# A hybrid state-space and attention layer on one core: spread row splits, moved sums, other queues for stores, a third weight set, two more dummy products

## The chip, the core and the metric

The kernel runs on one core of a Trainium2 chip. Five engines work side by side, each through its own instructions in order: TensorE (PE in the profile), VectorE (DVE), ScalarE (ACT), GpSimd (POOL) and SyncE (SP), which here only issues transfers between the chip's memory (DRAM) and on-chip memory. Engines and transfers wait for each other by semaphores. The metric is the device time of one execution in microseconds (us); lower is better.

## The reference

One step of a one-layer streaming encoder for 1024 prompt rows and 64 sample rows (T = 1088 columns in the kernel, which holds everything transposed), in float32. Cut to what matters:

```python
xn = rmsnorm(x, norm_mix_w)
z, xbc, dt, q, k, v, gate_ssm, gate_att = split(xn @ w_in)
xs, B, C = split(silu(causal_conv(xbc)))          # width 4
y = rmsnorm_groups((ssd_scan(xs, dt, B, C) + d * xs) * silu(z))
o = rmsnorm_heads(softmax(q1 k1) v - lam * softmax(q2 k2) v)   # 8 heads, rope on q and k
x = x + (sigmoid(gate_ssm) * (y @ w_ssm) + sigmoid(gate_att) * (o @ w_att)) @ w_out
ha, hb = split(rmsnorm(x) @ w_up)                  # 2 x 2816
x = x + (silu(causal_conv(ha)) * hb) @ w_down      # width 3
```

The caches of the sample stream enter attention, scan and convolutions; keys, values, states and convolution rows are outputs too.

## The kernel before, in words

*Products.* Each float32 operand is split into a rounded high part and the low rest, by a cast on ScalarE (`w_hi`, `hi`) and a subtraction on DVE (`w_lo`, `lo`). A product of two matrices is three passes: high by high, high by low, low by high (L159 to L161). The 1088 columns are cut into 384, 384 and 320 (`WIDE`). A product of 8 blocks of 128 and one such piece is 24 passes into one PSUM bank; an evacuation on ScalarE or DVE then frees the bank. Weights come as `w_f` by a load of 512 KB (L144), into pools with two sets; `extra`, where there is one, gives a third set, used in every third turn.

*Start.* The mean square of the input's rows is made on TensorE with a matrix of ones. Ahead of its products, products of ones by ones, whose result nothing reads, are put in by the table `IDLE`: nine ahead of the first mean square and eight behind it.

*Attention (some 350 to 1090 us).* Eight heads run over nine blocks of query rows. For each head SyncE loads `q_t`, the high and low keys `kh_t` and `kl_t` (three slots each), the caches `ch_t`, `cl_t`, `cv_t`, and the values `v_t`. Between the steps of attention a *filler* runs: the input projection's products for the gates (`gate_tiles`), for z (`z_tiles`) and for the convolution (`conv_tiles`), in the order of `ORDER`, at 1.9 pieces per step (`ATT_STEPS`). Their results go to DRAM as `g_sc`, `z_sc` and `x_sc`. The tiles `gt` and `zr` share three slots (`staged`). These stores are issued by SyncE in the same queue as the loads; only those of the first two entries of `ORDER` by GpSimd (`early`).

*Scan (some 1090 to 1350 us).* The state-space scan works over groups and chunks: loads of `in`, `zin` and, per chunk, a broadcast `bc` of 512 KB; exponentials on ScalarE, products on TensorE. The filler goes on between its steps, first the last z and gate tiles, then the two products that follow attention and the first ssm product. The second ssm product (`branch(stage, side, y_sc[D:], wbs[1], ...)`) comes behind the scan.

*FFN (some 1720 us to the end).* Up and down projections are made by a scheme with 7 products of blocks rather than 8. 22 *units* of the up projection (number i = 0 to 21 in the list `work`) each make one tile of `ha` and `hb`; 12 units of the down projection follow, in three groups of four (i = 22 to 25, 26 to 29, 30 to 33) over 8, 8 and 6 blocks of the 22. A unit has seven parts in the order b11, t2, b21, t3, t1, t4, b22, each for two halves s: 14 *piles* of products. A pile of the first two groups has 12 passes, of the last 9. The weights of the next unit are combined on GpSimd (`left_parts`, L1180 to L1193, tiles `ws`) and split. The hidden rows come back from DRAM (`q_sc`): *hidden sums* (`hidden_sums`, L1248 to L1251, tiles `gb`, `ge`) make the four t parts out of the four b parts, for one pair of tiles at a time, on GpSimd, with four loads and four stores; *hidden parts* (`hidden_part`, L1262 to L1264) load each part for a group (`hr`) and split it by a cast and a subtraction for each load. When the last unit of a group runs, the 14 parts of the next group are queued in `to_come` as the tiles that they go into become free, two after every second pile; `hidden_next` takes one from the queue after each pile and pins its instructions behind the last evacuations of PSUM (`emptied`).

*What sets the order.* A scheduler places the instructions of each engine by priorities and its own estimate of times; `tc.issue_after(x)` holds what is written under it behind x. A transfer from SyncE or ScalarE takes one of eight completion semaphores in turn and waits until the transfer before it on that semaphore has landed; the two engines share the eight. GpSimd's transfers have eight others.

Of the kernel before, what the change touches and what calls it, by code (L numbers as in the profile page):

```python
# [46 lines left out]
QR = 10  # L47
QSQ = 1
QUICK = 400
IDLE = (9, 8)  # L50
AT = 4
AHEAD_IN = 100
AHEAD = 100
# [23 lines left out]
def hybrid_layer(ctx: ExitStack, tc: tile.TileContext, xT, xN, prm, cst, rope, wvd, win, wbs, wba, wout, wup, wdn,  # L77
# [51 lines left out]

    xn = rows_by_part("xn")  # L130
    extra, turn, ahead, quick, asked, decayed, lowered = None, 0, AHEAD_IN, QUICK, None, None, None
    emptied, produced, early, early_w = (None, None), None, False, 0

    def raw_weights(block, k, m, pool=None):
        nonlocal turn, early_w
# [103 lines left out]
    def run(gen):  # L239
        for _ in gen:  # L240
            pass
# [349 lines left out]
    def gate_tiles(tiles):  # L591
        for j in tiles:
            def evac(ps, c, w):
                nonlocal last_gate
                gt = staged("gt")[:, :w]
                last_gate = act(gt, ps, AF.Tanh, scale=0.5)
                (G.dma_start if early else load)(out=g_sc[P * j : P * (j + 1), c : c + w], in_=gt)

            yield from project(win[B_G + j], evac)

    def z_tiles(tiles):
        for j in tiles:
            def evac(ps, c, w):
                zr = staged("zr")[:, :w]
                act(zr, ps, AF.Tanh, scale=0.5)
                V.scalar_tensor_tensor(zr, zr, 1.0, ps, ALU.add, ALU.mult)  # L606
                (G.dma_start if early else load)(out=z_sc[P * j : P * (j + 1), c : c + w], in_=zr)

            yield from project(win[B_Z + j], evac)

    def conv_tiles(tiles):
        for f in tiles:
            tail = None

            def evac(ps, c, w):
                nonlocal tail
                n = min(w, TP - c)
                pre = cv_pool.tile([P, 387], F32, name="pre", tag="pre", bufs=2)
                cc = cv_pool.tile([P, 384], F32, name="cc", tag="cc", bufs=3)
# [12 lines left out]
                cw = lambda i: col(O_CW + 4 * f + i)  # L632
                act(cc[:, :m], pre[:, :m], AF.Identity, bias=col(O_CB + f), scale=cw(0))  # L633
                for i in range(1, 4):
                    V.scalar_tensor_tensor(cc[:, :m], pre[:, i : i + m], cw(i), cc[:, :m], ALU.mult, ALU.add)  # L635
                act(pre[:, :m], cc[:, :m], AF.Tanh)
                V.scalar_tensor_tensor(cc[:, :m], pre[:, :m], 1.0, cc[:, :m], ALU.add, ALU.mult)
                load(out=x_sc[P * f : P * (f + 1), c : c + n], in_=cc[:, :n])
                if n < w:
                    load(out=x_sc[P * f : P * (f + 1), c + n : c + w], in_=cc[:, n + 3 : m])  # L640

            yield from project(win[B_X + f], evac)

    def stream():
        nonlocal early, early_w
        early_w = 10
        for n, (kind, which) in enumerate(ORDER):
            early = n < 2
# [16 lines left out]
    with (tc.tile_pool(name="ak", bufs=1) as ak, tc.tile_pool(name="at", bufs=1) as at,  # L665
# [159 lines left out]
        for h in range(8):  # L825
# [22 lines left out]
            run(last)  # L848
            late = [lambda h=h, o=o_t, q=ssq, s=s0: head_out(h, o, q, s)]
        late[0]()  # L850


    with (tc.tile_pool(name="sin", bufs=1) as sin, tc.tile_pool(name="sp", bufs=1) as sp,
# [183 lines left out]
    def mixed(m, c, t):  # L1037
        w = t.shape[1]
        for q in range(c // QW, -(-(c + w) // QW)):
# [2 lines left out]
            S.copy(hi, t[:, a - c : b - c])  # L1042
            V.tensor_tensor(out=lo, in0=t[:, a - c : b - c], in1=hi, op=ALU.subtract)

    run(branch(stage, side, y_sc[D:], wbs[1], 0, (n_sc, m_sc), mixed, parts, loaded))
    bs.release()
    xn_pool.release()

# [110 lines left out]
    def left_halves(blocks):  # L1159
# [6 lines left out]
        for h in range(2):  # L1166
            for r in range(2):
                yield own(halves[r][h])

    def left_parts(blocks, tag="fs"):  # L1170

        n = blocks[0].shape[1] // 2
        a = []
        for block in blocks:
# [14 lines left out]
        for i, src in enumerate((s1, q22)):  # L1189
            hi, lo = (x[:, 512 * i : 512 * i + n] for x in t)  # L1190
            split(hi, lo, src)
            yield hi, lo
        G.tensor_tensor(out=s2, in0=q12, in1=s2, op=ALU.subtract)  # L1193
        hi, lo = (wp.tile([P, WMAX], R32, name=name, tag=name, bufs=2)[:, :n] for name in ("w_hi", "w_lo"))
        split(hi, lo, s2)
        yield hi, lo
# [66 lines left out]
            S.copy(hi[:, j : j + n], t)  # L1263
            V.tensor_tensor(out=lo[:, j : j + n], in0=t, in1=hi[:, j : j + n], op=ALU.subtract)  # L1264

    to_come = []

    def hidden_next():
        if to_come:
            with tc.issue_after(emptied[0].ins), tc.issue_after(emptied[1].ins):  # L1270
                hidden_part(*to_come.pop(0))

    def piles(i, nk):
        banks = {}
# [208 lines left out]
    for i, (g, f) in enumerate(work[2:], 2):  # L1483
# [20 lines left out]
        for p, s in [(p, s) for p in ((0, 2, 1, 3, 4, 5, 6) if i == 2 else range(7)) for s in range(2)]:  # L1504
            u.send((p, s))
            hidden_next()
            if s == 1:
                more_left(i + 1)
                if last or i == FT - 2 and PARTS[p] in ("t2", "t3", "t4"):
                    to_come.extend((0 if i == FT - 2 else work[i + 1][0], PARTS[p], u) for u in range(2))  # L1510
                if p == 3 and i < FT + 2 and i % 2 == 0:
                    hidden_sums(i // 2 - 1)
        if i + 1 < len(work):
            left.setdefault(i + 1, []).extend(coming)
        del left[i]
# [108 lines left out]
```

## Time and profile before

| what | us |
|---|---|
| median of three runs | 2449.74 |
| lowest and highest of them | 2444.35, 2454.61 |
| the profiled execution | 2450.37 |
| its span | 2448.6 |
| TensorE busy in it | 2424.2 |
| DVE, ScalarE, GpSimd busy | 1603.0, 1141.4, 678.4 |

The profiled execution's own time is 1.8 us longer than its span, which runs from the first to the last recorded instruction. In the rows of a profile, L1283 is line 1283 of the kernel; `out<-in` names the tiles; PE is TensorE, SPq the queue of SyncE. "Idle before, releaser" is how long the engine did nothing ahead of the row and what ended that.

### The profile page before, as it was taken

How to read it: one execution, taken by the hardware profiler on the slowest of the kernel's cores; microseconds unless marked ns; L12 is line 12 of the kernel's file. 1: busy time of each engine (PE TensorE's matmuls, PEld its weight loads, DVE VectorE, ACT ScalarE, POOL GpSimd, SP SyncE). 2: the span in 40 equal slices, each digit the busy share in tenths (PEclk: the TensorE clock that was granted, in tenths of full speed). 3: DMA queues.
4: the chain of work that ended last, by engine and by line, in shares of the span. 5: the costliest groups of instructions: out<-in, count | busy, mean ns of one | idle time of the engine just before them, and what ended most of it. 6: DMA issues, size and time to landing. Idle time of an engine off the chain costs nothing.

```text
span 2448.6 us, 44619 instructions
## 1 busy us (share of the span) xinstructions
PE 2424.2 (99%) x16956; PEld 2351.5 (96%) x16956; DVE 1603.0 (65%) x2755; ACT 1141.4 (47%) x2497; POOL 678.4 (28%) x723
## 2 busy tenths in 40 slices
PE   9999999999999999999999999999999999999998
PEld 8999999999999999998889999999999999999998
DVE  7426255855787667546757784756877777786766
ACT  6334344644665555437664553224544433353542
POOL 0000011100100101004433334003366676655434
PEclk9999999999999999999999999999999999999999
DMA  4218158554444354255789765655143343467774
GB/s 173 82 57 290 61 208 270 148 154 142 126 149 131 116 158 121 91 170 173 218 261 318 226 193 186 196 182 181 54 143 126 121 139 116 153 206 202 212 185 155
DMA packets 267783, 403.55 MB, mean 165 GB/s; under 512 B 33296, under 2 KB 199696, under 8 KB 267440
## 3 DMA queue, kind: packets, MB, share of 16 engines
q1 hardware_dynamic: 254544, 376.99, 48.6%
q0 software_dynamic: 6960, 16.98, 3.4%
q10 hardware_dynamic: 6064, 6.72, 0.8%
q8 instruction: 133, 2.18, 0.4%
q14 instruction: 82, 0.67, 0.1%
HBM read 267.04 MB, written 133.56 MB: 164 GB/s over the span
## 4 chain that ended last, share of the span: by engine, by line
PE 90%; DVE 3%; DMA 3%; ACT 2%; issue 1%; POOL 0%; SPq 0%; ACTq 0%; DVEq 0%; POOLq 0%
PE mx L1283 17%; PE mm L159 13%; PE mm L161 13%; PE mm L160 12%; PE mm L1283 7%; PE mx L159 5%; PE mx L161 5%; PE mx L160 5%; PE po L776 3%; PE sc L729 2%; DMA hr<-q_sc 2%; PE sc L728 2%; PE pt L757 1%; PE mx L1343 1%; PE yi L902 1%
## 5 line engine op out<-in xcount | busy, mean ns | idle before, releaser
L159 PE MATMUL mm<-xn_hi,w_hi 128*128 128x384 f32 (+1 forms) x1416 | 471.0, 333 | 0.0
L161 PE MATMUL mm<-xn_hi,w_lo 128*128 128x384 f32 (+1 forms) x1416 | 468.3, 331 | 0.4 <-DVE w_lo L152 0.4
L160 PE MATMUL mm<-xn_lo,w_hi 128*128 128x384 f32 (+1 forms) x1416 | 467.7, 330 | 0.0
L159 PEld LDWEIGHTS mm<-xn_hi,w_hi 128*128 128x128 f32 x1416 | 266.7, 188 | 4.0 <-issue 1.6
L161 PEld LDWEIGHTS mm<-xn_hi,w_lo 128*128 128x128 f32 x1416 | 266.5, 188 | 3.7 <-issue 1.5
L160 PEld LDWEIGHTS mm<-xn_lo,w_hi 128*128 128x128 f32 x1416 | 266.7, 188 | 2.5 <-issue 1.1
L152 DVE TENSOR_TENSOR w_lo<-w_f,w_hi 128x1024 fp32r<-128x1024 f32 x116 | 147.0, 1269 | 110.0 <-ACT w_hi L151 109.4
L1283 PE MATMUL mx<-n,wh 128*128 128x272 f32 x1076 | 207.5, 290 | 0.7 <-ACT u L1427 0.5
L1283 PE MATMUL mx<-m,w_hi 128*128 128x272 f32 x1010 | 193.0, 289 | 4.6 <-DVE down L1441 4.6
L151 ACT CAST w_hi<-w_f 128x1024 fp32r<-128x1024 f32 x116 | 121.4, 1048 | 147.8 <-PE mm L160 89.8
L1283 PEld LDWEIGHTS mx<-n,wh 128*128 128x128 f32 x1076 | 170.5, 190 | 1.4 <-ACT u L1427 1.1
L1283 PEld LDWEIGHTS mx<-m,w_hi 128*128 128x128 f32 x1010 | 159.3, 189 | 5.3 <-issue 2.8
L1283 PE MATMUL mx<-n,wl 128*128 128x272 f32 x538 | 156.2, 290 | 0.0
L159 PE MATMUL mm<-b_hi,w_hi 128*128 128x384 f32 (+1 forms) x448 | 145.9, 327 | 0.6 <-DVE b_g L227 0.6
L1283 PE MATMUL mx<-m,w_lo 128*128 128x272 f32 x505 | 146.1, 289 | 0.0
L161 PE MATMUL mm<-b_hi,w_lo 128*128 128x384 f32 (+1 forms) x448 | 144.8, 324 | 0.6 <-DVE w_lo L152 0.6
L160 PE MATMUL mm<-b_lo,w_hi 128*128 128x384 f32 (+1 forms) x448 | 145.0, 324 | 0.0
L742 ACT ACTIVATE p_t<-sc,mx 128x1024 f32<-128x1024 f32 (+5 forms) x144 | 106.3, 739 | 75.9 <-DVE mx L733 34.1
L635 DVE SCALAR_TENSOR_TENSOR cc<-pre,par,cc 128x384 f32<-128x384 f32 (+1 forms) x216 | 126.4, 586 | 15.6 <-ACT cc L633 13.3
L623 POOL COPY pre<-pre 128x3 f32<-128x3 f32 x48 | 14.6, 304 | 353.5 <-DVE sm L745 121.7
L1068 ACT CAST w_hi<-ws 128x512 fp32r<-128x512 f32 (+1 forms) x62 | 37.6, 606 | 149.3 <-PE mx L1283 96.8
L159 PE MATMUL mx<-xn_hi,w_hi 128*128 128x384 f32 (+1 forms) x312 | 104.8, 336 | 2.2 <-DVE zr L606 2.2
(420 smaller groups left out, 6649.3 us busy)
## 6 DMA issues: line engine op xcount, KB each, us to landing
w_f<-in_win_dram SPq DMA_DIRECT2D x67, 512.0 KB, 4.0
w_f<-in_wup_dram SPq DMA_DIRECT2D x44, 512.0 KB, 3.8
hr<-q_sc SPq DMA_DIRECT2D x70, 272.0 KB, 5.0
bc<-a_sc SPq DMA_DIRECT2D x32, 512.0 KB, 5.9
q_sc<-hb SPq DMA_DIRECT2D x44, 272.0 KB, 2.3
gb<-q_sc SPq DMA_DIRECT2D x44, 272.0 KB, 3.7
x_sc<-cc SPq DMA_DIRECT2D x48, 192.0 KB, 1.9
q_sc<-gb SPq DMA_DIRECT2D x33, 272.0 KB, 2.4
```

The source lines that it names most:

```text
L151: S.copy(hi, w)
L152: lowered = V.tensor_tensor(out=lo, in0=w, in1=hi, op=ALU.subtract)
L159: PE.matmul(ps, a_hi, b_hi, start=i == 0, stop=False)
L160: PE.matmul(ps, a_hi, b_lo, start=False, stop=False)
L161: produced = PE.matmul(ps, a_lo, b_hi, start=False, stop=i == n - 1)
L635: V.scalar_tensor_tensor(cc[:, :m], pre[:, i : i + m], cw(i), cc[:, :m], ALU.mult, ALU.add)
L728: PE.matmul(ps[:n, a : a + b], lhs, r_hi, start=True, stop=False)
L729: PE.matmul(ps[:n, a : a + b], lhs, r_lo, start=False, stop=True)
L742: act(p_t[:n, :nk], sc[c][:n, :nk], AF.Exp, bias=mx[:n, c : c + 1], accum_out=dst)
L776: PE.matmul(po[:n, :P], a_t[b // 4][:kw, b % 4 * P : b % 4 * P + n], rhs, start=b == 0, stop=b == nb - 1)
L1068: S.copy(hi, src)
L1283: PE.matmul(ps, w[x][:, c], b[y][:, k], start=start and k == t == 0, stop=k == nk - 1 and t == 2, skip_group_check=not start)
```

## The change: what it does

Five edits. `IDLE` becomes (11, 8). The stores of the filler's tiles go through `send`: GpSimd until the end of attention, ScalarE after it. A pool `wx2` gives a third weight set during the second ssm product. The last hidden sums (the eleventh pair of tiles) leave the first unit of the down projection, behind its fourth part, for the third unit (i = 24), behind its sixth part, pinned behind the subtraction on GpSimd that ends that unit's weight sums. `hidden_next` lets two parts go for every three piles.

```diff
-IDLE = (9, 8)
+IDLE = (11, 8)
...
-    emptied, produced, early, early_w = (None, None), None, False, 0
+    emptied, produced, send, early_w = (None, None), None, G.dma_start, 0
...
-                (G.dma_start if early else load)(out=g_sc[P * j : P * (j + 1), c : c + w], in_=gt)
+                send(out=g_sc[P * j : P * (j + 1), c : c + w], in_=gt)
...
-                (G.dma_start if early else load)(out=z_sc[P * j : P * (j + 1), c : c + w], in_=zr)
+                send(out=z_sc[P * j : P * (j + 1), c : c + w], in_=zr)
...
-                load(out=x_sc[P * f : P * (f + 1), c : c + n], in_=cc[:, :n])
+                send(out=x_sc[P * f : P * (f + 1), c : c + n], in_=cc[:, :n])
                 if n < w:
-                    load(out=x_sc[P * f : P * (f + 1), c + n : c + w], in_=cc[:, n + 3 : m])
+                    send(out=x_sc[P * f : P * (f + 1), c + n : c + w], in_=cc[:, n + 3 : m])
...
         late[0]()
+        send = S.dma_start
...
+    extra = tc.alloc_tile_pool(name="wx2", bufs=1, side="right")
     run(branch(stage, side, y_sc[D:], wbs[1], 0, (n_sc, m_sc), mixed, parts, loaded))
+    extra.release()
+    extra = None
...
-        G.tensor_tensor(out=s2, in0=q12, in1=s2, op=ALU.subtract)
+        summed = G.tensor_tensor(out=s2, in0=q12, in1=s2, op=ALU.subtract)
...
+    to_come, owed = [], 0
...
     def hidden_next():
+        nonlocal owed
         if to_come:
-            with tc.issue_after(emptied[0].ins), tc.issue_after(emptied[1].ins):
-                hidden_part(*to_come.pop(0))
+            owed += 2
+            if owed >= 3:
+                owed -= 3
+                with tc.issue_after(emptied[0].ins), tc.issue_after(emptied[1].ins):
+                    hidden_part(*to_come.pop(0))
...
-                if p == 3 and i < FT + 2 and i % 2 == 0:
+                if p == 3 and i < FT and i % 2 == 0:
                     hidden_sums(i // 2 - 1)
+                elif (i, p) == (FT + 2, 5):
+                    with tc.issue_after(summed.ins):
+                        hidden_sums(FT // 2 - 1)
```

Over the whole program SyncE has 902 rows for 1079, GpSimd 784 for 647 and ScalarE 2006 for 1972. Lines behind the edits move by up to 13 (L1264 becomes L1270, L1441 becomes L1451).

The queue of SyncE in attention, where the loads of a head's queries and keys are issued. Before:

```order
L597 DMA g_sc<-gt 128x320
L144 DMA w_f<-in_win_dram 128x1024
L672 DMA kh_t<-k_st 64x1088
L672 DMA q_t<-q_st 64x1088 x2
L672 DMA kh_t<-k_st 64x1088
L672 DMA kl_t<-k_st 64x1088 x2
L672 DMA q_t<-q_st 128x1088
L672 DMA kh_t<-k_st 64x1088 x2
L597 DMA g_sc<-gt 128x384
L672 DMA kl_t<-k_st 64x1088 x2
L597 DMA g_sc<-gt 128x384
L692 DMA cv_t<-in_cv_dram 128x4x128
```

The same place in the queue of SyncE now:

```order
L144 DMA w_f<-in_win_dram 128x1024
L671 DMA kh_t<-k_st 64x1088
L671 DMA q_t<-q_st 64x1088 x2
L671 DMA kh_t<-k_st 64x1088
L671 DMA kl_t<-k_st 64x1088 x2
L671 DMA q_t<-q_st 128x1088
L671 DMA kh_t<-k_st 64x1088 x2
L671 DMA kl_t<-k_st 64x1088 x2
L691 DMA cv_t<-in_cv_dram 128x4x128
```

The three stores of `g_sc` have left it; the loads keep their order among themselves.

The queue of GpSimd in the first units of the down projection, where the weight sums (`ws`, `w_f`), the hidden sums (`ge`, `gb`) and the adding stores of the results (`down`) stand. Before:

```order
L1180 TENSOR_TENSOR ws_24596<-w_f 128x512
L1448 DMA out_dram<-down 128x544
L1181 TENSOR_TENSOR ws_24597<-ws_24596,w_f 128x512
L1186 TENSOR_TENSOR w_f<-w_f 128x512
L1248 TENSOR_TENSOR ge<-gb_24720,gb_24719 128x544
L1193 TENSOR_TENSOR ws_24597<-w_f,ws_24597 128x512
L1249 TENSOR_TENSOR gb_24720<-gb_24722,gb_24720 128x544
L1250 TENSOR_TENSOR gb_24719<-gb_24722,ge 128x544
L1448 DMA out_dram<-down 128x544 x2
L1251 TENSOR_TENSOR gb_24721<-gb_24721,gb_24719 128x544
L1448 DMA out_dram<-down 128x544
```

The same place now, up to the hidden sums two units later:

```order
L1187 TENSOR_TENSOR ws_24593<-ws_24592,w_f 128x512
L1192 TENSOR_TENSOR w_f<-w_f 128x512
L1199 TENSOR_TENSOR ws_24593<-w_f,ws_24593 128x512
L1458 DMA out_dram<-down 128x544 x3
L1186 TENSOR_TENSOR ws_24858<-w_f 128x512
L1187 TENSOR_TENSOR ws_24859<-ws_24858,w_f 128x512
L1192 TENSOR_TENSOR w_f<-w_f 128x512
L1199 TENSOR_TENSOR ws_24859<-w_f,ws_24859 128x512
L1254 TENSOR_TENSOR ge<-gb_25264,gb_25263 128x544
L1458 DMA out_dram<-down 128x544
L1255 TENSOR_TENSOR gb_25264<-gb_25266,gb_25264 128x544
```

The hidden sums no longer stand between the first down unit's weight sums, but behind those of the third.

The queue of SyncE at the start of the last group of the down projection, with loads of the hidden parts (`hr`), of earlier results (`xr`) and of weights (`w_f`). Before:

```order
L1262 DMA hr<-q_sc 128x544
L1262 DMA hr<-q_sc 128x272
L1417 DMA xr<-out_dram 128x544 x4
L1176 DMA w_f<-in_wdn_dram 128x768
L1262 DMA hr<-q_sc 128x544
L1262 DMA hr<-q_sc 128x272
L1262 DMA hr<-q_sc 128x544
L1262 DMA hr<-q_sc 128x272
L1417 DMA xr<-out_dram 128x544
```

The same place now:

```order
L1268 DMA hr<-q_sc 128x544
L1268 DMA hr<-q_sc 128x272
L1427 DMA xr<-out_dram 128x544 x4
L1268 DMA hr<-q_sc 128x544
L1268 DMA hr<-q_sc 128x272
L1182 DMA w_f<-in_wdn_dram 128x768
L1268 DMA hr<-q_sc 128x544
L1268 DMA hr<-q_sc 128x272
L1268 DMA hr<-q_sc 128x544
L1268 DMA hr<-q_sc 128x272
L1268 DMA hr<-q_sc 128x544
L1268 DMA hr<-q_sc 128x272
```

Behind the four loads of `xr` there stood the loads of two hidden parts; now six follow, the last two (rows behind those shown) around a store of `down`.

More of the change, by code (lines that the diff above doesn't have):

```diff
@@ L637, in evac @@
                 V.scalar_tensor_tensor(cc[:, :m], pre[:, :m], 1.0, cc[:, :m], ALU.add, ALU.mult)
-                load(out=x_sc[P * f : P * (f + 1), c : c + n], in_=cc[:, :n])
+                send(out=x_sc[P * f : P * (f + 1), c : c + n], in_=cc[:, :n])
                 if n < w:
-                    load(out=x_sc[P * f : P * (f + 1), c + n : c + w], in_=cc[:, n + 3 : m])
+                    send(out=x_sc[P * f : P * (f + 1), c + n : c + w], in_=cc[:, n + 3 : m])
             yield from project(win[B_X + f], evac)
     def stream():
-        nonlocal early, early_w
+        nonlocal early_w
         early_w = 10
-        for n, (kind, which) in enumerate(ORDER):
-            early = n < 2
+        for kind, which in ORDER:
             yield from {"c": conv_tiles, "z": z_tiles, "g": gate_tiles}[kind](which)
@@ L1168, in left_halves @@
                 yield own(halves[r][h])
+    summed = None
     def left_parts(blocks, tag="fs"):
+        nonlocal summed
         n = blocks[0].shape[1] // 2
@@ L1264, in hidden_part @@
             V.tensor_tensor(out=lo[:, j : j + n], in0=t, in1=hi[:, j : j + n], op=ALU.subtract)
-    to_come = []
+    to_come, owed = [], 0
     def hidden_next():
+        nonlocal owed
         if to_come:
-            with tc.issue_after(emptied[0].ins), tc.issue_after(emptied[1].ins):
-                hidden_part(*to_come.pop(0))
+            owed += 2
[3 more added lines that the diff above has]
+                    hidden_part(*to_come.pop(0))
     def piles(i, nk):
```

## Prediction

> **What bounds the kernel now.** I read the page first (busy shares and the chain of work that ended last), then the waits of TensorE, then the granted clock in stretches of 50 us, then the rows around each wait.
>
> ```profile
> span 2448.6 us, 44619 instructions
> ...
> PE 2424.2 (99%) x16956; PEld 2351.5 (96%) x16956; DVE 1603.0 (65%) x2755; ACT 1141.4 (47%) x2497; POOL 678.4 (28%) x723
> ...
> POOL 0000011100100101004433334003366676655434
> ...
> PE 90%; DVE 3%; DMA 3%; ACT 2%; issue 1%; POOL 0%; SPq 0%; ACTq 0%; DVEq 0%; POOLq 0%
> ```
>
> TensorE is busy for 2424.2 of 2448.6 us and is 90% of the chain. The work is a list of products that the change leaves as it is, so an edit can win only what TensorE loses between them: 24.4 us of idle time, and what a lower clock adds to the busy time. The profiled execution took 2450.4 us, span 2448.6; it lies 0.7 us above the median of the three runs, 2449.7. The runs spread from 2444.4 to 2454.6, so I call 0.5%, 12.2 us, the limit of what can be told from no change: faster means under 2437.5, slower over 2462.0.
>
> The waits of TensorE (total, times, longest, in us) that the change can reach:
>
> ```profile
> PE mx L1283 <- DVE down L1441: 4.6, 2, 2.6
> ...
> PE mx L159 <- DVE zr L606: 2.2, 1, 2.2
> ...
> PE st L315 <- DVE ns L315: 1.1, 1, 1.1
> ...
> PE mm L161 <- DVE w_lo L152: 1.0, 2, 0.6
> ```
>
> Two waits of the down projection, 2.6 and 2.0 us, are the largest. Some waits cost twice. Stretches of 50 us (the first number behind the five busy times is the granted clock):
>
> ```profile
> 500.00:550.00 50.00, 47.59 (x299) 44.85 (x298) 27.28 (x58) 22.81 (x66) 1.10 (x2) 0.97 0.57 154
> ...
> 1100.00:1150.00 50.00, 47.76 (x343) 42.10 (x343) 33.34 (x38) 35.18 (x90) 23.58 (x16) 1.00 0.54 168
> ...
> 2200.00:2250.00 50.00, 48.00 (x368) 47.57 (x368) 36.56 (x48) 18.44 (x36) 27.70 (x24) 0.97 0.87 236
> ...
> 2350.00:2400.00 50.00, 47.26 (x365) 46.84 (x364) 38.72 (x73) 23.93 (x54) 19.20 (x18) 0.97 0.85 234
> ```
>
> TensorE in attention (start, length, in brackets the idle time before and its releaser):
>
> ```profile
> 532.22 0.47 PE L728 MATMUL sc<-kh_t,q_t 128*128 128x512 f32 x1 [1.08 <-DMA kh_t<-k_st]
> ...
> 532.87 0.34 PE L159 MATMUL mm<-xn_hi,w_hi 128*128 128x384 f32 x1
> ...
> 533.04 0.34 PE L160 MATMUL mm<-xn_lo,w_hi 128*128 128x384 f32 x1
> ...
> 534.88 0.60 PE L729 MATMUL sc<-kl_t,q_t 128*128 128x512 f32 x1 [1.33 <-DMA kl_t<-k_st]
> ...
> 536.13 0.52 PE L159 MATMUL mm<-xn_hi,w_hi 128*128 128x384 f32 x1
> ...
> 536.45 0.52 PE L160 MATMUL mm<-xn_lo,w_hi 128*128 128x384 f32 x1
> ```
>
> Before the second wait, products of 384 columns start 0.17 us apart, behind it 0.32: the clock is halved. A granted 0.97 over 50 us means 0.03 x 50 = 1.5 us lost. So two waits of together 2.4 us at 531 to 535 cost 3.9 us, and each of the two large waits of the down projection, which also lie in stretches at 0.97, costs 1.5 us more than itself. The single wait of 2.2 us at 1107 (scan start, below) lies in a stretch at 1.00 and costs only itself.
>
> The Trainium skill, "TensorE: Matmul & The Clock Gate", section "Why this matters for your kernels", tells a kernel to avoid idle gaps of TensorE above some 3 us, since one idle window sends the clock to half. By that rule none of these gaps would cost clock time, and removing two of them would bring 3.0 us less than I count below, a sum of -2.4 rather than -5.4. The trace disagrees: gaps of 2.0 to 2.6 us, and two of 1.1 and 1.3 close together, have a halved clock behind them. I go by the rows.
>
> **The change, part by part.**
>
> *Two more dummy products.* They stand ahead of the first mean square, in a gap:
>
> ```profile
> 1.64 3.62 PE L315 MATMUL st<-ones 128*128 128x128 f32 x16
> ```
>
> Sixteen records take 3.62 us, 0.226 each; a product is two records, so two products add 0.90 us. They end at 5.26 + 0.90 = 6.16, ahead of the 6.33 at which the 1.1 us wait for ns (quoted above) ends. DVE hides them; were it 0.2 us faster they would cost up to 0.9. Cost taken 0; gain at most a half-clock stretch of 1.5, if they keep one away. I see none that they would, so 0.
>
> *Filling stores from GpSimd.* In attention SyncE's rows lose the stores of g, z and x. At 531 this is the queue of SyncE, then its waits from 505 to 535:
>
> ```profile
> 526.57 1.93 SPq L672 DMA_DIRECT2D kh_t<-k_st  x2
> ...
> 529.55 0.33 SPq L597 DMA_DIRECT2D g_sc<-gt  x1
> ...
> 530.70 1.64 SPq L672 DMA_DIRECT2D kl_t<-k_st  x2
> ...
> SPq L597 <- DMA q_t<-q_st: 1.0, 1, 1.0
> ...
> SPq L672 <- DMA q_t<-q_st: 0.8, 1, 0.8
> ```
>
> The kh_t loads were issued before the g_sc store, so the first wait (1.08, kh_t) stays. The kl_t loads come behind it, the second ending 532.34. Both the store and the loads waited for a q_t transfer to land: each DMA here waits for the one eight places earlier in a ring of eight completion semaphores, which SyncE and ScalarE share. Without the store, the kl_t loads move one place up in that ring, about one issue earlier: 530.70 - 529.55 = 1.15. I take 1.2 off the 1.33 wait. The remaining idle time, 1.1 + 0.1, is well below the 2.0 that halved it elsewhere, so its 1.5 goes as well: -2.7. Bounds: 0 if kl_t lands no earlier because kh_t's packets are still moving, -3.9 if both waits go. What comes to GpSimd: by the order 784 rows for 647, nearly all DMA issues, at this price (min, median, max ns):
>
> ```profile
> L597 POOL DMA_DIRECT2D g_sc<-gt x6: 539/540/552, 328.1 to 348.8; - x6
> ```
>
> 137 x 0.54 = 74 us on an engine which is nearly idle until the scan (its tenths above), so 0. If a store there waits for its tile, the small copies of the convolution behind it wait too; one product of 24 passes at 0.17 us per pass (4.1 us) hides that.
>
> *Stores from ScalarE in the scan.* The wait of 2.2 us is at the scan's start, where z tiles have three slots and a slot is free when its store has landed:
>
> ```profile
> 1080.86 12.76 SPq L872 DMA_DIRECT2D bc<-a_sc  x5
> ...
> 1099.51 0.44 ACT L605 ACTIVATE zr<-mm 128x320 f32<-128x320 f32 x1 [5.79 <-DMA z_sc<-zr]
> ...
> SPq L607 <- DVE zr L606: 46.7, 12, 6.1
> ```
>
> Five broadcast loads take SyncE 12.8 us to issue, because they wait for places in the ring; the z stores come behind them, and ScalarE waits 5.8 us for a slot. Now ScalarE issues these stores itself. It is free of SyncE's place in line, but its store waits for the same ring, and ScalarE's next tanh, casts and evacuations stand behind it in order, so the wait for a landed load holds ScalarE rather than SyncE. I take 0: the wait is replaced by one like it. Bounds: -2.2 if it goes; and if all nine z stores hold TensorE as this one did, 9 x 2.2 = +20.
>
> *Third weights for the second ssm product.* It removes a wait for w_lo, one of the two, 0.6 at the longest. -0.6, bounds 0 and -1.0. SBUF alone is spent.
>
> *Last sums moved.* In the first unit of the down projection (rows of DVE, then of GpSimd):
>
> ```profile
> 2208.10 0.71 DVE L1264 TENSOR_TENSOR m<-hr,m 128x544 fp32r<-128x544 f32 x1
> ...
> 2213.59 4.56 DVE L1264 TENSOR_TENSOR m<-hr,m 128x544 fp32r<-128x544 f32 x1 [1.18 <-ACT m L1263]
> ...
> 2219.38 3.42 DVE L1069 TENSOR_TENSOR wl<-w_f,wh 128x512 fp32r<-128x512 f32 x2
> ...
> 2215.91 1.65 POOL L1248 TENSOR_TENSOR ge<-gb,gb 128x544 f32<-128x544 f32 x1
> ```
>
> A split of a hidden part, 0.71 us alone, took 4.56 while GpSimd ran its weight sums and then the first of the hidden sums (1.65); two weight splits took 3.42. DVE's evacuations stand behind them, and TensorE waits 2.0 us with 1.5 of clock behind. The hidden sums go to a unit with no hidden parts to split. Earlier units run the same sums beside weight splits and no such wait is among the largest, so I take the whole: -3.4. Bounds: 0, because GpSimd's weight sums stay and the paced parts still meet them, and -3.4.
>
> *Pacing.* Two parts per three piles rather than one per pile moves five or six of 14 parts (with their loads, casts and subtractions) behind the boundary into the next unit. At the last boundary before (SyncE, ScalarE, GpSimd, TensorE):
>
> ```profile
> 2377.81 0.33 SPq L1176 DMA_DIRECT2D w_f<-in_wdn_dram  x1
> ...
> 2378.80 2.68 SPq L1262 DMA_DIRECT2D hr<-q_sc  x4
> ...
> 2386.78 0.97 ACT L1263 CAST m<-hr 128x544 fp32r<-128x544 f32 x2 [6.48 <-DMA hr<-q_sc]
> ...
> 2385.27 1.02 POOL L1180 TENSOR_TENSOR ws<-w_f 128x384 f32<-128x384 f32 x1 [2.67 <-DMA w_f<-in_wdn_dram]
> ...
> 2387.95 1.49 POOL L1186 TENSOR_TENSOR w_f<-w_f 128x384 f32<-128x384 f32 x1
> ...
> 2388.22 0.29 PE L1283 MATMUL mx<-m,w_lo 128*128 128x272 f32 x1
> ...
> 2388.60 0.28 PE L1283 MATMUL mx<-m,w_lo 128*128 128x272 f32 x1
> ```
>
> Then, two parts were left, loaded at 2378.8, cast 8.0 us later; DVE waited behind the cast, and TensorE lost 2.6. Now six are left. Three passes take 0.38 us, so a pile of nine takes 1.14. The two b22 parts are released behind piles 8 and 9 and used at 13 and 14: four piles, 4.6 us, less 0.4 for the evacuation that releases them, leaves 4.2. Loads are thinner than before, so the landing is below 8.0; even at 4 us, with 1.0 for two casts and 0.7 for a subtraction, it is 5.7, late by 1.5. At 8.0 it is late by 5.5. The first b22 load also needs a slot that two additions of GpSimd free, which now stand behind the three weight sums (1.0 to 1.5 each), themselves behind a weight load (7.5 us from 2377.81 to 2385.27). I take the middle, 3.5, clock loss as before: 3.5 - 2.6 = +0.9. At the boundary before that a pile is 12 passes, 1.5 us, the lead 5.7: as long as the least that is needed, so half the 0.7 that a landing of 4.7 would miss, +0.4. Pacing: +1.3, between -4.1 (2.6 + 1.5, all gone) and +5.
>
> Sum: 0 - 2.7 + 0 - 0.6 - 3.4 + 1.3 = -5.4. From 2450.4 that is 2445.0, and as a median, 0.7 lower, 2444.3.
>
> **The rivals.**
>
> *All the waits go.* 3.9 (attention) + 2.2 (scan) + 0.6 + 3.4 + 4.1 = 14.2, so 2435.5. For it: each is caused by something late in one queue, and each edit touches that queue. Against it: kh_t was not behind a store, and b22's lead falls from some twelve piles to four.
>
> *The stores gain nothing.* The kl_t loads still land only when kh_t's have, so the 2.7 stays lost, and the scan is as it was. Then -5.4 + 2.7 = -2.7, or, with half the sums' gain also lost to GpSimd's weight sums, -1.0: 2447 to 2449. The q_t waits of SyncE, which are waits for landing and not for issue, speak for it; the store that stood ahead speaks against. The Trainium skill, "DMA: Bandwidth & Descriptors", section "Issuing engines are not separate DMA queues", would have it so too: DMAs of several engines share the same 16 engines, and issuing from more than one saves only issue time.
>
> *Slower: ScalarE held at its stores.* SyncE spent 46.7 us in 12 waits for zr, 3.9 each. If ScalarE spends that in its own queue in the scan, where it is busy for 35.2 of 50 us, the exponentials and evacuations behind are late. At 2.2 us lost per z store, nine times, the result is 2444.3 + 20 = 2464. It decides from (17.7 us)/9 = 2.0 us per store. Against it: the stores of gates wait for no DVE, and TensorE has other products of the filling to run.
>
> **How the numbers follow.** The sum as worked out 0.50, all waits gone 0.24, no gain from the stores 0.11, ScalarE held 0.15. The sum's own range is 2438 to 2452 (pacing and sums at their ends). Over all cases 2431 to 2458 leaves out most of the last one and a little below: under 2 in 10. Faster: 0.24 and 0.03 of the likeliest case; slower: 0.15 and 0.01; the rest is within 0.5%.
>
> **What would show it.** Right: the wait for kl_t and the halved clock at 535 gone, kh_t's still listed; no wait for down in the first down unit and clock 1.00 there; the first b22 cast of the last group waiting for hr, and TensorE for a b22 split, by 2 to 5 us; ScalarE with waits for DMA ahead of evacuations at the scan's start. Wrong: clock at 1.00 from 2350 to 2400 (pacing works), or waits of TensorE for zr, gt or tr scattered over the scan (ScalarE held), or new waits in attention for the convolution's tiles (GpSimd held).

## The result, and the profile after

| | median, us | lowest and highest | ratio to before, 95% interval |
|---|---|---|---|
| before | 2447.19 | 2444.35, 2454.61 | |
| changed | 2459.23 | 2455.66, 2467.60 | 1.0055 [1.0042, 1.0067] |

The changed kernel is slower by some 12 us. That is 0.5%, about what the prediction called the limit of what can be told; the interval lies wholly above 1, and its centre just beyond the limit. The forecast was 2444.3, and the median lies just above the 2431 to 2458 that the prediction gave over all its cases. The profiled executions show most of the difference: spans of 2457.5 and, before, 2448.6, 8.9 us apart. The page of the changed kernel:

```profile
core 0 of [0], span 2457.5 us
...
PE 2424.8 (99%) x16960; PEld 2349.7 (96%) x16960; DVE 1603.6 (65%) x2755; ACT 1139.4 (46%) x2497; POOL 753.1 (31%) x865
```

TensorE is as busy as before (2424.8 us; before 2424.2); its idle time is 2457.5 - 2424.8 = 32.7 us, before 24.4. So 8.3 of the 8.9 us are new idle time. Its waits (total, times, longest, in us), the largest:

```profile
PE mm L1293 <- DVE down L1451: 3.1, 2, 1.7
...
PE sc L728 <- DMA kl_t<-k_st: 2.9, 2, 1.6
...
PE mx L1293 <- DVE down L1451: 2.3, 3, 1.0
...
PE yi L902 <- DVE y L910: 1.8, 1, 1.8
...
PE pt L797 <- DVE ol L801: 1.6, 1, 1.6
...
PE mm L1293 <- DVE m L1270: 1.2, 3, 0.7
...
PE mx L1293 <- DVE m L1270: 1.1, 2, 0.7
...
PE mx L1293 <- ACT down L1445: 1.1, 1, 1.1
```

The wait for `zr` (2.2) is gone, and the two large waits of the down projection (2.6, 2.0) are. In their place the FFN has more of them, of up to 1.7 each. Stretches (five busy times, granted clock, DMA share, GB/s):

```profile
500.00:550.00 50.00, 47.77 (x310) 45.15 (x309) 27.40 (x58) 22.94 (x67) 5.45 (x12) 1.00 0.55 155
...
1050.00:1100.00 50.00, 48.37 (x291) 46.20 (x291) 17.03 (x42) 14.79 (x35) 2.71 (x5) 0.97 0.57 183
...
2200.00:2250.00 50.00, 47.19 (x368) 46.07 (x367) 38.38 (x57) 22.22 (x42) 24.97 (x21) 1.00 0.67 185
...
2250.00:2300.00 50.00, 47.15 (x373) 46.62 (x372) 30.62 (x53) 21.22 (x42) 21.58 (x19) 1.00 0.78 215
...
2350.00:2400.00 50.00, 48.18 (x379) 47.30 (x378) 33.55 (x64) 22.18 (x49) 19.99 (x20) 1.00 0.72 181
```

The clock is 1.00 in the three stretches that the prediction named at 0.97. But 2250 to 2300, where TensorE was busy for 49.39 before, now has 2.85 us of idle time. Compared at equal work done by TensorE (the start of the same product in both traces), the changed kernel is 2.2 us ahead at 550, level within 0.5 at 775 (the longer of the two waits for `kl_t`, 1.6 near 611, is new), 3.9 behind at 1271 (two more new waits: 1.6 for `ol` before 1100, with a clock of 0.97, and 1.8 for `y`), 2.6 behind after the second ssm product, and then loses 6.8 in the FFN up to 2400; the last stretch gives 0.5 back.

### The profile page after: what moved, and what is told of

Same layout as the page of the kernel before. It is cut to its first block, busy times and chain, and to the rows that moved or that the text cites. A ratio compares the mean times of both kernels' runs of the same rounds, so it can differ in the third digit from the quotient of the medians.

```text
span 2457.5 us, 44636 instructions
## 1 busy us (share of the span) xinstructions
PE 2424.8 (99%) x16960; PEld 2349.7 (96%) x16960; DVE 1603.6 (65%) x2755; ACT 1139.4 (46%) x2497; POOL 753.1 (31%) x865
## 5 line engine op out<-in xcount | busy, mean ns | idle before, releaser
L638 POOL DMA_DIRECT2D x_sc<-cc x72 | 39.0, 542 | 259.7 <-DVE cc L637 189.1
L144 POOL DMA_DIRECT2D w_f<-in_win_dram x9 | 5.1, 561 | 327.7 <-DVE w_lo L152 327.7
```

The costliest lines, as they stand in the source:

```text
L144: (G.dma_start if early_w > 0 else load)(out=w, in_=block.rearrange("p (k m) -> p k m", k=k))
L638: send(out=x_sc[P * f : P * (f + 1), c : c + n], in_=cc[:, :n])
```

## Experiments: each edit alone

Two theories stood at the start. *Hidden parts:* the paced parts are late and cost some 7 us, the moved sums give back what they win, the rest costs 2. *Stores:* the stores from ScalarE and GpSimd cost most of it. Each edit was run alone on the kernel before, and those ahead of the FFN also together (hunks of the change, cut).

**Sums.**

```diff
-                if p == 3 and i < FT + 2 and i % 2 == 0:
+                if p == 3 and i < FT and i % 2 == 0:
                     hidden_sums(i // 2 - 1)
+                elif (i, p) == (FT + 2, 5):
```

> Only the move of the last hidden sums to the third down unit; all else as before. Theory A (the moved sums cost the time: their four loads and four stores now lie among the weight loads of the third and fourth down unit and hold slots that the row splits need): about 4 to 7 us slower than before, with GpSimd waiting some 10 us for a weight load near 2260 and waits of TensorE near 2268. Theory B (the pacing costs it, the sums are a gain as forecast): 2 to 3.5 us faster than before, the wait for down near 2221 gone.

**Pacing.**

```diff
+            owed += 2
+            if owed >= 3:
+                owed -= 3
```

> Only the pacing of the row splits. Theory A: within 2 us of before, as splits that come later still come in time. Theory B: 4 to 7 us slower, with new waits of TensorE for splits of hidden parts (m) or evacuations behind them in the first unit of each group (near 2191, 2313 and 2396).

**Stores.**

```diff
-                (G.dma_start if early else load)(out=z_sc[P * j : P * (j + 1), c : c + w], in_=zr)
+                send(out=z_sc[P * j : P * (j + 1), c : c + w], in_=zr)
...
+        send = S.dma_start
```

> Only the filling stores, from GpSimd in attention and from ScalarE in the scan. Theory A (what is won at 531 comes back at later head changes and in the scan): 3 to 6 us slower than before, with waits of 1.6 us for kl_t near 609, for ol near 1088 and for y near 1271. Theory B (those waits come from chance or from the other edits): within 1 us of before or up to 3 faster.

**Dummies, stores and third weights together** (the edits ahead of the FFN).

```diff
+IDLE = (11, 8)
...
+        send = S.dma_start
...
+    extra = tc.alloc_tile_pool(name="wx2", bufs=1, side="right")
```

> The three edits ahead of the FFN together (dummy products, filling stores, third weights), pacing and sums as before. If the parts add up, this is the run with the stores alone less 1.3 us for the third weights, and less 0 for the dummy products; together with the two FFN edits it makes the 12 us of the change, so 4 to 6 us slower than before if the FFN edits cost 6 to 8.

**Third weights alone, dummies alone.**

```diff
+    extra = tc.alloc_tile_pool(name="wx2", bufs=1, side="right")
```

> Only the third weight set in the second ssm product. By the prediction's step 0.6 us faster (0 to 1.0), by the profile of the changed kernel 1.3, with the waits for b_g and w_lo near 1557 gone; below what the runs can tell either way.

```diff
-IDLE = (9, 8)
+IDLE = (11, 8)
```

> Only the two more dummy products. By the prediction's step no change: they fill part of the wait for ns near 5 us. If they delay the first mean square, up to 0.9 us slower; if they keep a half-clock stretch away, 1.5 us faster.

| edits made | median, us | ratio to before, 95% interval |
|---|---|---|
| sums | 2447.74 | 1.0005 [0.9996, 1.0014] |
| pacing | 2454.99 | 1.0032 [1.0020, 1.0044] |
| stores | 2449.60 | 1.0009 [1.0000, 1.0018] |
| dummies, stores, third weights | 2448.42 | 1.0006 [0.9998, 1.0015] |
| third weights | 2447.74 | 1.0001 [0.9992, 1.0011] |
| dummies | 2447.49 | 0.9999 [0.9991, 1.0008] |

Before was run beside each: 2447.24 beside the first four, 2447.91 beside the last two. Pacing is the main cause: 0.32 of the sum of 0.46% (-0.01 + 0.01 + 0.09 + 0.05 + 0.32), and the only edit whose interval lies clear of 1. The whole is 0.55%; the 0.09 between them lie within the intervals, and whether the edits disturb each other by some 2 us is not settled. Within 2180 to 2450 the waits of TensorE add to 5.1 us before, 7.5 with the sums moved, 11.2 paced, 12.2 in the changed kernel.

## Experiments: where the moved sums give it back

The wait at 2221 is gone in the kernel with the sums alone, as forecast. Another takes its place at 2258. Here are the two longest waits of SyncE from 2230 to 2256, then rows of SyncE, GpSimd and TensorE:

```profile
SPq L1256 <- POOL ge L1251: 13.8, 1, 13.8
SPq L1265 <- DMA q_sc<-gb: 6.9, 3, 3.7
```

```profile
2242.96 6.52 SPq L1265 DMA_DIRECT2D hr<-q_sc  x3
...
2249.53 14.81 SPq L1179 DMA_DIRECT2D w_f<-in_wdn_dram  x3
...
2254.65 1.31 POOL L1183 TENSOR_TENSOR ws<-w_f 128x512 f32<-128x512 f32 x1 [10.99 <-DMA w_f<-in_wdn_dram]
...
2258.32 0.52 PE L1286 MATMUL mx<-m,w_hi 128*128 128x272 f32 x2 [0.89 <-ACT down L1438]
...
2261.80 0.52 PE L1286 MATMUL mm<-m,w_hi 128*128 128x272 f32 x2 [1.71 <-DVE down L1444]
```

The tiles `gb` and `ge` of the sums come from the same eight slots (`fb`) as the loaded parts `hr`. Moved to the third unit, the sums take five of them just when SyncE already fetches parts of the next group. These loads wait 6.9 us for the sums' stores to land, and in SyncE's queue the weights of the next unit stand behind them: GpSimd waits 11 us for `w_f`, and TensorE loses 0.9 and 1.7. (The 13.8 us are SyncE's wait, ahead of this, for GpSimd to make `ge`, the first of the sums.) The changed kernel shows the wait of GpSimd too:

```profile
2264.82 1.30 POOL L1186 TENSOR_TENSOR ws<-w_f 128x512 f32<-128x512 f32 x1 [10.50 <-DMA w_f<-in_wdn_dram]
```

To tell "the weights' place behind the parts" from "the sums' own work", the weights were moved out of that queue in two ways.

**Weights from GpSimd** (alone, with the sums, with the pacing).

```diff
-    def left_parts(blocks, tag="fs"):
+    def left_parts(blocks, tag="fs", start=load):
...
-            load(out=w[:, : 2 * n], in_=block)
+            start(out=w[:, : 2 * n], in_=block)
```

The weights of the down projection then pass `start=G.dma_start`.

> Only the weight loads of the down projection issued by GpSimd. Theory A: before has the same holding up at the last boundary only, so 0 to 3 us faster. Theory B: GpSimd's issue price beside its sums makes it 0 to 3 us slower.

> The moved sums, and the weight loads of the down projection issued by GpSimd rather than SyncE; all else as before. Theory A (the sums' tiles hold slots, the row-split loads that wait for those slots stand ahead of the weight load in SyncE's queue, and so the weights of the fourth down unit come some 10 us late): GpSimd's wait for the weight load near 2255 falls from 11 us to under 4, the waits of TensorE of 0.9 and 1.7 near 2260 go, and the time is 2 to 4 us below before. Theory B (the loss there is contention between DVE and GpSimd): no more than 1 us from the run with the moved sums alone.

> The pacing, and the weight loads of the down projection issued by GpSimd; all else as before. Theory A (the paced loads hold up the weight loads behind them in SyncE's queue): of the 7.8 us that pacing costs, some 3 to 5 go; the waits for splits of about 2 us in the last group stay. Theory B (the splits themselves are late): 6 to 9 us slower than before, as with SyncE.

Measured: 1.0025 [1.0016, 1.0034] alone, 1.0017 [1.0009, 1.0026] with the sums, 1.0049 [1.0036, 1.0062] with the pacing. The instrument itself costs 6 us, so this could not separate the theories. Its price per load, from the groups by line (min, median, max ns), is small:

```profile
L1176 POOL DMA_DIRECT2D w_f<-in_wdn_dram x24: 546/585/863, 2166.5 to 2414.7; - x24
```

SyncE's median for the same loads, before, is 0.332 us. 24 x (0.585 - 0.332) is 6 us of GpSimd's time, and its loads now stand behind GpSimd's waits for DVE. TensorE's waits from 2180 to 2450 add to 6.7 us in the profile with this edit alone, 5.1 before; where the rest was lost was not traced.

**Weights first in SyncE's queue.** The parts are held behind the last weight load that is written ahead of them.

```diff
-            load(out=w[:, : 2 * n], in_=block)
+            fetched = load(out=w[:, : 2 * n], in_=block)
...
-            with tc.issue_after(emptied[0].ins), tc.issue_after(emptied[1].ins):
+            with tc.issue_after(emptied[0].ins), tc.issue_after(emptied[1].ins), tc.issue_after(fetched.ins):
```

> Before, with each row-split load pinned in SyncE's queue behind the weight loads that the program issued ahead of it; sums and pace as before. Theory A (loads that wait for slots hold the weights): little to gain where before has no late weights, within 1.5 us of before. Theory B: the same.

> The moved sums, with the row-split loads pinned behind the weight loads (all still from SyncE). Theory A: GpSimd's wait of 11 us for the weight load near 2255 falls under 5, TensorE's waits of 0.9 and 1.7 near 2260 go and with them the half clock, so 2 to 4 us below before. Theory B (contention of DVE and GpSimd, or the load's own landing): the waits near 2260 stay and the time is within 1 us of the run with the moved sums alone.

> The pacing, with the row-split loads pinned behind the weight loads. Theory A (weights late behind waiting loads make up half of the 7.8 us): 3 to 5 us slower than before, the wait of 1.8 near 2412 smaller. Theory B (the splits and the evacuations behind them on DVE are late by themselves): 7 to 9 us slower.

Measured: 1.0015 [1.0007, 1.0024] alone, 0.9999 [0.9990, 1.0007] with the sums, 1.0047 [1.0035, 1.0059] with the pacing. With the sums, GpSimd at the same place, and the waits of TensorE from 2180 to 2300:

```profile
2250.08 1.30 POOL L1183 TENSOR_TENSOR ws<-w_f 128x512 f32<-128x512 f32 x1 [5.05 <-DVE u L1432]
```

```profile
PE mx L1286 <- DVE down L1444: 0.9, 1, 0.9
...
PE mm L1286 <- DVE down L1444: 0.2, 1, 0.2
```

GpSimd no longer waits for a load there, and TensorE's 2.6 us near 2260 are gone (the 0.9 left is at the first boundary, near 2219). SyncE's wait for `ge` is still there, 15.3 us now, so it alone does not make the weights late: the loads of parts ahead of them in the queue were the cause of the wait at 2258. The order itself costs 3.9 us by the medians when it comes alone; its profile shows a new wait of TensorE of 1.2 near 2306, and the rest of that cost was not traced. On top of it the sums win 0.16%, 3.6 us, close to the 3.4 forecast, and the two cancel. That the queue is the whole of the giveback rests on this difference of two ratios, each known to some 0.09%.

## Experiments: the pacing

In the kernel paced alone, the first boundary: ScalarE and DVE, SyncE, GpSimd, DVE, TensorE; below it DVE, SyncE and GpSimd before.

```profile
2200.17 1.20 ACT L1263 CAST n<-hr 128x544 fp32r<-128x544 f32 x2 [1.74 <-DMA hr<-q_sc]
...
2200.85 1.36 DVE L1264 TENSOR_TENSOR n<-hr,n 128x544 fp32r<-128x544 f32 x2 [1.28 <-ACT n L1263]
...
2208.40 0.68 DVE L1069 TENSOR_TENSOR wl<-w_f,wh 128x512 fp32r<-128x512 f32 x1
...
2204.97 2.53 SPq L1262 DMA_DIRECT2D hr<-q_sc  x5
...
2207.60 0.37 SPq L1176 DMA_DIRECT2D w_f<-in_wdn_dram  x1
...
2209.10 0.33 SPq L1176 DMA_DIRECT2D w_f<-in_wdn_dram  x1
...
2216.01 1.73 POOL L1180 TENSOR_TENSOR ws<-w_f 128x512 f32<-128x512 f32 x1 [4.51 <-DMA w_f<-in_wdn_dram]
...
2220.58 2.42 DVE L1069 TENSOR_TENSOR wl<-ws,wh 128x512 fp32r<-128x512 f32 x1 [1.91 <-ACT wh L1068]
...
2223.28 3.41 DVE L1069 TENSOR_TENSOR wl<-w_f,wh 128x512 fp32r<-128x512 f32 x2
...
2223.41 0.52 PE L1287 MATMUL mx<-m,w_hi 128*128 128x272 f32 x2 [1.52 <-DVE down L1445]
...
2227.19 0.49 PE L1287 MATMUL mx<-m,w_hi 128*128 128x272 f32 x2 [2.00 <-DVE down L1445]
```

```profile
2203.51 0.68 DVE L1069 TENSOR_TENSOR wl<-w_f,wh 128x512 fp32r<-128x512 f32 x1
...
2204.72 0.39 SPq L1176 DMA_DIRECT2D w_f<-in_wdn_dram  x1
...
2211.47 1.38 POOL L1180 TENSOR_TENSOR ws<-w_f 128x512 f32<-128x512 f32 x1 [4.86 <-DMA w_f<-in_wdn_dram]
```

The parts now due later are late: ScalarE waits 1.7 us for their loads, and DVE 1.3 for ScalarE's cast. DVE works in order, so its splits of the current unit's weights, which stand behind, are late as well: the one shown begins at 2208.4 rather than 2203.5. The load of the next unit's weights takes the slot that this split frees, so it is issued at 2209.1 rather than 2204.7. (Five loads of parts stand ahead of the weights in SyncE's queue, three before; they take 2.5 us rather than 1.6, so they alone do not explain the 4.4.) GpSimd begins the weight sums at 2216.0 rather than 2211.5, DVE gets its split of them late (2.42 and 3.41 for one and two splits; one took 0.68 at 2215), the evacuations of `down` stand behind it, and TensorE loses 1.5 and 2.0 where it had lost one wait of 1.9. At the last boundary (TensorE, GpSimd, ScalarE, TensorE):

```profile
2391.78 0.39 PE L1287 MATMUL mm<-m,w_hi 128*128 128x272 f32 x1 [1.03 <-DVE m L1264]
...
2407.76 1.03 POOL L1180 TENSOR_TENSOR ws<-w_f 128x384 f32<-128x384 f32 x1 [2.15 <-DMA w_f<-in_wdn_dram]
...
2409.91 0.51 ACT L1068 CAST wh<-ws 128x384 fp32r<-128x384 f32 x1 [8.85 <-POOL ws L1181]
...
2413.73 0.49 PE L1287 MATMUL mm<-m,w_hi 128*128 128x272 f32 x2 [1.83 <-DVE down L1445]
```

First TensorE waits for late splits (1.6 in all in the products into `mm`, 1.0 the longest), then for evacuations behind the split of the next weights, which come late too (1.8; GpSimd began these sums at 2401.7 before). At the boundary between these two TensorE loses 1.2, waiting for `w_hi`, and 0.5.

**One boundary at a time.**

```diff
-            owed += 2
+            owed += 2 if i <= FT else 3
```

> Pacing only for the row splits of the down projection's first group; one per pile at the two later boundaries, all else as before. Theory A (the loss sits where the paced loads meet the last hidden sums and the late weight load, at the first boundary): 3 to 5 us slower than before, and the lines behind 2300 as before. Theory B (the loss sits at the last boundary, where the piles are short and the lead for b22 is 4 us): within 1.5 us of before.

```diff
-            owed += 2
+            owed += 2 if i > FT else 3
```

> Pacing only for the second and third group. Theory A: 2 to 4 us slower than before, with the first boundary as before (one wait of about 2 us near 2221). Theory B: 6 to 8 us slower, the whole of the pacing's cost.

Measured: 2452.36, 1.0019 [1.0010, 1.0027], for the first; 2449.04, 1.0008 [0.9999, 1.0017], for the two later ones; before 2447.90 beside both. So by the medians 4.5 us of it come at the first boundary (2.4 to 6.6 by the interval) and about 1 at the later two (0 to 4), 5.6 together for the 7.8 of the whole.

Weights first, above, does not save the pacing: 1.0047, and 1.0015 for the order alone, so the pacing costs 0.32% there as well. In its profile GpSimd has the weights in time (it begins their sums at 2210.3), the splits of the parts are late, and TensorE loses at the first boundary

```profile
2224.07 0.79 PE L1290 MATMUL mx<-m,w_hi 128*128 128x272 f32 x2 [4.88 <-DVE down L1448]
```

So late weights are not needed for the loss; late splits of parts, with the evacuations behind them on DVE, are enough. How much of their lateness is the late load and how much DVE slowed beside GpSimd was not told apart.

**The changed kernel without pacing.**

```diff
-            owed += 2
-            if owed >= 3:
-                owed -= 3
```

> The changed kernel with one row split per pile, as before; the four other edits stay. If pacing costs 7.8 us here too, 4 us slower than before; if pacing and the moved sums make each other worse, as the four parts together (9.5) fall short of the change's 12, this run is 1 to 2 us slower than before, or the same.

2451.51, 1.0015 [1.0006, 1.0024]: without the pacing, 0.40% of the 0.55 is gone. The rest, 0.15, agrees within the intervals with the sums and the edits ahead of the FFN (0.05 + 0.06). With the table above, this shows from both sides that the pacing is the main cause.

## Experiments: the stores

The edit of the stores has two halves. In the scan, with the stores alone (ScalarE, DVE, TensorE):

```profile
1265.52 0.33 ACTq L597 DMA_DIRECT2D g_sc<-gt  x1
...
1265.89 1.05 ACT L151 CAST w_hi<-w_f 128x1024 fp32r<-128x1024 f32 x1 [6.16 <-DMA b_hi<-o_sc]
...
1266.97 1.23 DVE L152 TENSOR_TENSOR w_lo<-w_f,w_hi 128x1024 fp32r<-128x1024 f32 x1 [5.51 <-ACT w_hi L151]
...
1270.14 1.10 PE L902 MATMUL yi<-bc,xx 128*64 128x128 f32 x16 [1.83 <-DVE y L910]
```

ScalarE ends its tanh at 1259.7 and issues the store of it only at 1265.5: it waits for a place in the ring, held by a load of SyncE (`b_hi`). The cast of the next weights stands behind it (6.2 us idle), DVE's subtraction behind the cast, `y` behind that, and TensorE loses 1.8; the stretch 1250 to 1300 has a clock of 0.97.

**Stores from GpSimd in attention, from SyncE in the scan as before.**

```diff
+        send = load
```

> Filling stores from GpSimd in attention, and from SyncE again in the scan. Theory A (attention wins 1 to 3 us, ScalarE's stores in the scan lose 3): 1 to 3 us faster than before, no wait for y near 1271, and the wait for zr near 1107 back or less. Theory B (GpSimd's stores land later and cost as much at the head changes): within 1 us of before or slower, with waits for kl_t near 609 and others up to 780.

Measured: 2444.99, 0.9991 [0.9981, 1.0001], against 1.0009 with both halves. The cast that waited 6.2 us there, here:

```profile
1257.82 1.04 ACT L151 CAST w_hi<-w_f 128x1024 fp32r<-128x1024 f32 x1 [0.30 <-PE mm L160]
```

The wait of TensorE for `y` at L910 is listed in all four kernels with stores from ScalarE (1.8, 2.2, 2.1, 1.8) and in none of the other sixteen, before among them. A wait for `ol` near 1087 (1.6, 0.9, 0.5, 0.4) is in the same four and in no other. So ScalarE's half costs some 0.18%, 4.6 us by the medians. GpSimd's half wins 0.09%, 2.4 us, which its interval does not quite tell from nothing. It has a price too: all seven kernels with stores from GpSimd in attention have a second wait for `kl_t` near 609, of 0.2 to 1.6 us, and none of the other thirteen has it; its cause was not traced.

## Experiments: what is left when the losing parts go

**Sums, third weights, stores from GpSimd in attention only; with the weights first, and without.**

```diff
+        send = load
...
+    extra = tc.alloc_tile_pool(name="wx2", bufs=1, side="right")
...
+                elif (i, p) == (FT + 2, 5):
```

> Third weights, filling stores from GpSimd in attention alone (SyncE in the scan), moved sums with the row-split loads behind the weight loads; no pacing, dummy products as before. If the parts add up (2.4 for the stores, 1.2 for the weights, 2 to 4 for the sums): 5 to 8 us faster than before, so about 2440 to 2442.

> Third weights, filling stores from GpSimd in attention alone, moved sums; without the pin of row-split loads behind the weight loads. If the pin costs as much as it did alone (3.7) also here, 6 to 9 us faster than before; if it is worth what it removed beside the moved sums, 2 to 4 us faster, less than the combined kernel with it.

2442.32, 0.9985 [0.9976, 0.9993], with; 2443.82, 0.9981 [0.9972, 0.9990], without, each beside its own runs of before. Both are faster than the kernel before and the changed one, and cannot be told from each other. Alone, the three edits add to -0.03% (0.05 + 0.01 - 0.09) and not to -0.19; the intervals just allow that, and why they win more together is not shown.

## Why the prediction was wrong, step by step

The steps that failed are, by size, the cost of the pacing (the +1.3 of the sum, measured +7.8), the stores in the scan (0, measured +4.6) and the last sums (-3.4, measured about 0).

- *What bounds the kernel:* right, TensorE's idle time and its clock; 8.3 of the 8.9 us in the profiles are idle time. But "an edit can win only what TensorE loses" has another side that the sum hardly used: an edit can lose more than that.
- *Dummies, 0:* right (0.9999).
- *Third weights, -0.6:* the waits for `w_lo` fall from 1.0 to 0.4; 1.0001 is too coarse to tell 0.6 from nothing.
- *Stores in attention, -2.7:* alone, -2.4, with an interval that reaches 0. The size agrees, and by luck: the 1.2 of it that was to come from the wait did not come. The step "Without the store, the kl_t loads move one place up in that ring, about one issue earlier" failed. In the changed kernel (SyncE, TensorE):

```profile
530.04 1.48 SPq L671 DMA_DIRECT2D kl_t<-k_st  x2
...
532.42 0.47 PE L727 MATMUL sc<-kh_t,q_t 128*128 128x512 f32 x1 [0.94 <-DMA kh_t<-k_st]
...
535.06 0.47 PE L728 MATMUL sc<-kl_t,q_t 128*128 128x512 f32 x1 [1.29 <-DMA kl_t<-k_st]
```

 The loads are issued at 530.04 rather than 530.70, and the wait is 1.29 rather than 1.33: the landing didn't move. Over all profiles this wait is 0.8 to 1.3 us in the seven kernels without the store and 0.9 to 1.4 in the thirteen with it. What went is the halved clock, 1.5 us, with 0.2 us less of idle time. The rival that said so of kl_t ("still land only when kh_t's have") was right there. That the stores did away with the halved clock is not shown by one trace: the stretch from 500 to 550 has a clock of 1.00 in all seven kernels without the store, but also in five of the thirteen with it, and 0.97 in the other eight.
- *Stores in the scan, 0:* failed at "the wait is replaced by one like it". The mechanism that the prediction gave to its slower rival (ScalarE held, its casts behind it) is what happens, seen at one gate store rather than at nine z stores: +4.6 where the bounds were -2.2 and +20. The wait shown and the clock behind it are 3.3 of that; the rest was not traced.
- *Last sums, -3.4:* the wait went, as forecast. "The hidden sums go to a unit with no hidden parts to split" failed: none is split there, but parts are already loaded, into the slots that the sums take, and the weights stand behind those loads. Measured +0.05% instead, between -0.04 and +0.14. The bounds had 0 as the worst, and nothing had excluded a loss.
- *Pacing, +1.3:* measured +7.8, beyond the bound of +5. The lateness of b22's splits was right in kind and over-sized (in the changed kernel TensorE waits 2.3 us in all for `m`, over both later boundaries, against 3.5 at the last alone; the 2.6 and its clock are gone). What failed is the count of boundaries: the two later ones were costed, and the first, with twelve-pass piles, was not. It gives some 4.5 of it. What stands behind the late splits was also left out, at every boundary: DVE's evacuations, and the splits that free the slots of the next weights. And the sign that the text gave for a pacing that works, a clock of 1.00 from 2350 to 2400, appeared while the pacing lost: it watched one boundary.
- *The chances:* slower had 0.16, nearly all of it on ScalarE. The slower case that came was another: late splits of paced parts that hold DVE's evacuations and the next weights, where the text had only the opposite direction (weights delaying the slots of b22). ScalarE's stores, priced there at up to 20, cost some 4.6.

## What to carry to other kernels

When work is moved to a later place, list what stands behind it on every in-order engine and queue that it passes, and at every place where the pattern repeats, not at the worst one alone: here the evacuations and the next weights stood behind the parts, and the boundary that was not looked at cost most. Before work is put into a quiet stretch, look at whose slots it takes and what is being prefetched into them then, since an engine may be free and its buffers not. And a store that an engine issues for itself can make that engine wait for another queue's transfer, as ScalarE did here for a load of SyncE (5.8 us), so put it on one that has nothing urgent behind it.

## What the runs showed that was not expected

- Gaps and the clock. The length of a gap alone doesn't tell. Before, 2.0 us at 2221 had a stretch at 0.97 and 2.2 at 1107 one at 1.00; paced, 1.5 and 2.0 within 4 us leave 1.00 (first line below); with the sums, 3.1 us goes with 0.93 (second line):

```profile
2200.00:2240.00 40.00, 35.24 (x272) 34.13 (x271) 31.13 (x42) 17.94 (x33) 21.97 (x19) 1.00 0.85 254
```

```profile
2350.00:2400.00 50.00, 46.26 (x347) 45.85 (x346) 36.79 (x70) 23.04 (x52) 18.67 (x18) 0.93 0.87 240
```

 The Trainium skill, "TensorE: Matmul & The Clock Gate", section "Why this matters for your kernels", warns of gaps above some 3 us. The 3.1 agrees with it; the 2.0 before does not, and it is no safe line.
- Waits for landings are not the same in every profiled execution. Kernels whose attention and scan are those of before list a wait for `zr` between none and 2.2 us, for kh_t between none and 1.1, and four of them one of 0.6 to 2.8 for `y` at another chunk (L912). So the 2.2 that the prediction wanted to explain was probably in part that execution's own.
- Twenty-four weight loads moved from SyncE's queue to GpSimd's cost 6 us in all, though GpSimd was busy for only 28% of the span before.
